# Low parts of the second feed-forward stage's down and plain weights: an adding transfer from GpSimd's queue instead of a VectorE subtraction

## The chip, the cores and the metric

The kernel runs on one core of a Trainium2 chip. The metric is the device time of one execution in microseconds. The kernel before took 1125.16 us (median of three runs, 1124.86 to 1127.51); lower is better.

## The reference

One step of a hybrid decoder layer in fp32, for 512 prompt tokens and 8 x 4 sample tokens that share all weights:

```
x = x + 1/2 * SwiGLU_1(RMSNorm(x))
h = RMSNorm(x); z = h @ w_in          # attention heads and mLSTM heads work on z
x = x + concat(A, B) @ w_out
x = x + 1/2 * SwiGLU_2(RMSNorm(x))

def _swiglu(x, w_gate, w_up, w_down):
    return (jax.nn.silu(x @ w_gate) * (x @ w_up)) @ w_down
```

The model width is 1024, the hidden width of the feed-forward stages 2816. The change lies in SwiGLU_2 alone, the last stage of the kernel.

## The kernel before

All activations are kept transposed: a tile holds 128 features in its partitions and all 544 tokens along its rows, in two halves of 272.

**Products in three passes.** To keep nearly fp32 accuracy with fast matrix products, every weight tile and every activation tile is split into a high part (rounded to the type fp32r) and a low part (the value less its high part). A product is then three matmul passes: high weight by high activation, high weight by low activation, low weight by high activation. The low part of the weights is read last of the three, for each of the (up to) eight blocks of 128 rows in turn.

**Raw tiles and jobs.** `Raw` (line 493) is one weight transfer from DRAM: eight blocks of 128 rows by 256 columns, 1 MB, into a tile `wraw` of which there are three buffers. It feeds two `Job`s (line 521), one for each 128 columns. `Job.split` (line 528) makes the two parts of its 128 columns: ScalarE casts to the high part `whi`, VectorE subtracts to get the low part `wlo`. Both come from one ring of eight buffers (`wsp`), so four jobs' weights fit. A job is then 48 matmuls (three passes, eight blocks, two halves of the tokens), 36 where it has six blocks.

**The second feed-forward stage** (`ffn_jobs`, line 717, called with "ffn2" at line 1803) goes through the 22 hidden blocks of 128 features in three parts of 8, 8 and 6 (`PARTS`, line 28). In each part, hidden blocks are made first (gate and up products, Silu, product), then added into all eight output blocks by eight down jobs. The first four hidden blocks (`PLAIN`, line 29) are made by plain jobs: two gate jobs and two up jobs for two blocks, eight jobs in all. All later ones are made by `Fast` jobs (line 555), a seven-product scheme on 2 x 2 blocks whose weight sums are made on VectorE; a fast job is seven units of 24 matmuls, each with its own split of weights, and has a separate loader and splitter. So the order of the stage is: eight plain jobs, two fast jobs, eight down jobs; four fast, eight down; three fast, eight down (six blocks each).

**What sets the order.** The program is written out by a planner at build time. `Order` (line 52) keeps a model clock of each engine and when each tile is ready; generators ("threads") are resumed when their model time has come, and emit their instructions. `run` (line 602) holds two of them: the loader, which issues the load of raw tile n on SP's queue when both jobs of raw tile n - 3 have been split, and the splitter, which splits a job's weights when TensorE is four units (two jobs) ahead of it, or three units where the job before is a fast one. Each engine then runs its own instructions in the order in which they were emitted, and waits on semaphores for what it needs. GpSimd issues nothing and computes nothing in this stage.

In the part that the change touches, the split reads:

```
src = self.raw.t[:, :nk, self.c * P:(self.c + 1) * P]
act.copy(hi[:, :nk], src)
yield R(hi) - 0.3
dve.tensor_tensor(lo[:, :nk], src, hi[:, :nk].bitcast(F32), op=OP.subtract)
self.raw.left -= 1
```

`yield R(hi) - 0.3` lets other threads go on until the model has `hi` ready.

Of the kernel before, what the change touches and what calls it, by code (L numbers as in the profile page):

```python
# [8 lines left out]
F32 = mybir.dt.float32  # L9
F32R = mybir.dt.float32r  # L10
AF = mybir.ActivationFunctionType
OP = mybir.AluOpType
# [4 lines left out]
P = 128  # L17
# [34 lines left out]
class Order:  # L52
# [26 lines left out]
    def done(self, *tiles, kind="aux"):  # L79
        for p in tiles:  # L80
            self.free[kind].append(self.used[p.tensor.name][0] + 0.2)
# [58 lines left out]
    def R(self, *aps):  # L140
        return max(self.ready.get(a.tensor.name, (0.0, ""))[0] for a in aps) + 0.2
# [103 lines left out]
def hybrid_layer_kernel(ctx: ExitStack, tc: tile.TileContext, I: dict, C: dict, O: list):  # L245
    nc = tc.nc
# [10 lines left out]
    od = Order()  # L257
    act, dve, pool = Engine(od, "act", nc.scalar), Engine(od, "dve", nc.vector), Engine(od, "pool", nc.gpsimd)
    dma = Engine(od, "dma", nc.sync)
    dma2 = pool  # L260
    R, U, done = od.R, od.U, od.done

    def halves(ap):
        return ap.rearrange("p (a b) -> p a b", a=2)
# [10 lines left out]
    def t2(name, shape=(P, N), dt=F32):  # L275
        return gp.tile(list(shape), dt, name=name, tag="t2", bufs=NT2)
# [33 lines left out]
    class Norm:  # L310
        def __init__(self, g0):
            self.g0 = g0
            self.x = [None] * KD
            self.begun = self.n = 0
            self.rows = False
            self.rb = None
# [49 lines left out]
    class FastNorm(Norm):  # L366
# [58 lines left out]
        def split(self, name, j, t):  # L425
            hi, lo = t2("oh", (P, 2, HN), F32R), t2("ol", (P, 2, HN), F32R)
            yield R(t) - 0.3
            act.copy(hi, t)
            yield R(hi) - 0.3
            dve.tensor_tensor(lo, t, hi.bitcast(F32), op=OP.subtract)  # L430
            self.ops[(name, j)] = (hi, lo)
# [61 lines left out]
    class Raw:  # L493


        def __init__(self, w, r0, nk, cols, *more):
            self.w, self.cols = w, cols
            self.parts = [(r0, nk)] + list(more)
            self.nk = sum(n for _, n in self.parts)
            self.left = len(cols)  # L500
            self.t = None

        def load(self):
            self.t = wp.tile([P, 8, 256], F32, name="wraw", tag="wraw", bufs=3)
# [1 line left out]

        def load_cols(self):
            c0, n = self.cols[0], len(self.cols)
            together = all(c == c0 + i * P for i, c in enumerate(self.cols))
            k0 = 0  # L510
            for r0, nk in self.parts:
                rows = self.w[r0:r0 + nk * P]
                if together:
                    dma.dma_start(self.t[:, k0:k0 + nk, :n * P], rows[:, c0:c0 + n * P].rearrange("(k p) c -> p k c", p=P))
                else:
                    for i, c in enumerate(self.cols):
                        dma.dma_start(self.t[:, k0:k0 + nk, i * P:(i + 1) * P],
                                      rows[:, c:c + P].rearrange("(k p) c -> p k c", p=P))
                k0 += nk

    class Job:
# [6 lines left out]
        def split(self):  # L528
            hi = wp.tile([P, 8, P], F32R, name="whi", tag="wsp", bufs=8)
            lo = wp.tile([P, 8, P], F32R, name="wlo", tag="wsp", bufs=8)  # L530
            nk = self.nk
            if self.custom:
                self.custom(hi, lo)
            else:
                src = self.raw.t[:, :nk, self.c * P:(self.c + 1) * P]
                act.copy(hi[:, :nk], src)
                yield R(hi) - 0.3
                dve.tensor_tensor(lo[:, :nk], src, hi[:, :nk].bitcast(F32), op=OP.subtract)
                self.raw.left -= 1
            self.w = (hi, lo)  # L540

# [175 lines left out]
    def ffn_jobs(pre, get_norm, after):  # L717
        wg, wu, wd = I[pre + "_w_gate"], I[pre + "_w_up"], I[pre + "_w_down"]
        jobs = []
        for f0, f1 in zip(PARTS, PARTS[1:]):  # L720
# [4 lines left out]
            def gate(f, zg=zg):  # L725
                def post(ps, full):
                    z = t2("zg")
                    yield 0, 0, lambda: get_norm().rb is not None
                    dve.tensor_tensor(halves(z), ps, halves(get_norm().rb), op=OP.mult)
                    done(full, kind="mm")  # L730
                    yield R(z) - 0.5
                    act.activation(z, z, AF.Silu)
                    zg[f] = z
                return post
# [9 lines left out]
            def up(f, zg=zg, hidden=hidden):  # L744
                def post(ps, full):
                    z = t2("zu")
                    yield 0, 0, lambda: zg[f] is not None
                    dve.tensor_tensor(halves(z), ps, halves(get_norm().rb), op=OP.mult)
                    done(full, kind="mm")
                    yield R(z) - 0.3  # L750
                    dve.tensor_tensor(z, zg[f], z, op=OP.mult)
                    yield from hidden(f, z)
                return post
# [63 lines left out]
            op = lambda name, k: get_norm().op(name, k)  # L817
            for f in range(0, nf, 2):
                c0 = (f0 + f) * P
                if f0 + f >= PLAIN:  # L820
                    jobs.append(Fast(Halves((wg, wu), 0, c0), Halves((wg, wu), 4 * P, c0), op, both(f)))
                    continue
                cols = [c0, c0 + P]
                ru = Raw(wu, 0, 8, cols)
                if jobs or f0 or f:
                    rg = [Raw(wg, 0, 8, cols)] * 2
                    jobs += [Job(rg[i], i, xs, gate(f + i)) for i in range(2)]
                else:
                    jobs += [Job(Raw(wg, 0, 8, [cols[i]]), 0, xs, gate(f + i)) for i in range(2)]
                jobs += [Job(ru, i, xs, up(f + i)) for i in range(2)]  # L830

            def down(m, last=f1 == NF):
                def post(ps, full):
                    dve.scalar_tensor_tensor(halves(xT[m]), ps, 0.5, halves(xT[m]), op0=OP.mult, op1=OP.add)
                    done(full, kind="mm")
                    if last:
                        yield from after(m)
                    yield 0
                return post

            for m in range(0, KD, 2):
                r = Raw(wd, f0 * P, nf, [m * P, (m + 1) * P])
                for c in range(2):
                    jobs.append(Job(r, c, lambda k, hs=hs: hs[k], down(m + c)))
        return jobs

    n1, n2, n3 = FastNorm(0), Norm(8), FastNorm(16)

    jobs = ffn_jobs("ffn1", lambda: n1, n2.add)

    last_fast = max(n for n, j in enumerate(jobs) if isinstance(j, Fast))
# [905 lines left out]
    for m in range(0, KD, 2):  # L1757
        r = Raw(w_out, 4 * P, 3, [m * P, (m + 1) * P])
        jobs += [Job(r, i, lambda k: mixed[4 + k], wo(m + i, False)) for i in range(2)]
    for m in range(0, KD, 2):  # L1760
        r = Raw(w_out, 0, 4, [m * P, (m + 1) * P], (7 * P, 1))
# [19 lines left out]
    def last_half(h, ps):  # L1781
# [19 lines left out]
        dma.dma_start(yp[:, 2 * h:2 * h + 2, m * P:(m + 1) * P], yt)  # L1801

    jobs += ffn_jobs("ffn2", lambda: n3, store)

    def late():
# [90 lines left out]
```

## Time and profile before

| | us |
|---|---|
| median of three runs | 1125.16 |
| the profiled execution | 1127.17 |
| its span, first to last instruction | 1125.4 |
| TensorE busy (matmul) | 1102.8 |
| VectorE busy | 768.4 |
| ScalarE busy | 504.3 |
| GpSimd busy | 95.6 |

The page and the views come from one profiled execution. PE is TensorE's matmuls and PEld its weight loads, DVE is VectorE, ACT ScalarE, POOL GpSimd, SP the engine that issues the loads; "SPq" marks such an issue, and its duration is the issue's own, not the transfer's. Nearly every instruction has line L223 or L282, the helpers that record it, so groups are told apart by the tiles that they write and read: `wlo<-wraw,whi` writes a low part from a raw tile and a high part. A bracket behind a row of a timeline is the idle time of the engine before it and who ended it. Matmuls are pipelined, so a single one lasts longer (about 0.29 us) than the step from one to the next (about 0.125 us).

### The profile page before, as it was taken

To read this page: it belongs to the slowest core of one execution; us is meant where nothing else is said; L and a number is where in the kernel's file an instruction comes from. 1 tells how busy PE (TensorE), PEld (TensorE's weight loads), DVE (VectorE), ACT (ScalarE), POOL (GpSimd) and SP (SyncE) were. 2 spreads that over 40 slices of the span, in tenths; PEclk is the share of its full clock that TensorE was granted. 3 is DMA by queue.
4 is the path that set the end of the run, shared out by engine and by line. 5 is a ranking of instruction groups with operands and counts; after the bars stand their busy time and mean duration, and the time that the engine had idled before them with its cause. 6 is when DMAs were issued, how large, how long until landed. Compare 5 with 4: busy or idle time off the path is not lost. (4 is left out here: it accounts for less than half of the span.)

```text
span 1125.4 us, 21401 instructions
## 1 busy us (share of the span) xinstructions
PE 1102.8 (98%) x8819; PEld 1050.6 (93%) x8819; DVE 768.4 (68%) x1232; ACT 504.3 (45%) x900; POOL 95.6 (8%) x105
## 2 busy tenths in 40 slices
PE   7999999999999999999989999999999999999998
PEld 6999999999999999988876869999999999999997
DVE  6888337873487678689786537778962687537752
ACT  5555215451245446455653535454541355314541
POOL 0000000000000000165563010000000000000000
PEclk9999999999999999999999999999999999999999
DMA  7305312432143465675979563342242122422232
GB/s 231 102 15 159 105 38 76 149 114 78 36 140 99 124 215 134 189 227 161 316 227 331 189 215 113 97 148 76 76 134 92 61 91 75 150 76 76 66 105 60
DMA packets 143229, 145.34 MB, mean 129 GB/s; under 512 B 8868, under 2 KB 120772, under 8 KB 143132
## 3 DMA queue, kind: packets, MB, share of 16 engines
q1 hardware_dynamic: 143068, 143.98, 41.2%
q8 instruction: 69, 1.13, 0.4%
q14 instruction: 28, 0.23, 0.1%
q0 software_dynamic: 64, 0.00, 0.0%
HBM read 132.54 MB, written 9.18 MB: 126 GB/s over the span
## 5 line engine op out<-in xcount | busy, mean ns | idle before, releaser
L223 ACT CAST whi<-wraw 128x1024 fp32r<-128x1024 f32 (+3 forms) x180 | 174.1, 988 | 121.0 <-PE mm L282 93.5
L223 DVE TENSOR_TENSOR wlo<-wraw,whi 128x1024 fp32r<-128x1024 f32 (+3 forms) x180 | 210.2, 1176 | 20.4 <-ACT whi L223 20.2
L282 PE MATMUL mm<-oh,wlo 128*128 128x272 f32 x720 | 209.3, 291 | 2.2 <-DVE wlo L223 2.0
L282 PE MATMUL mm<-oh,whi 128*128 128x272 f32 x720 | 207.6, 288 | 0.1
L282 PE MATMUL mm<-ol,whi 128*128 128x272 f32 x720 | 207.2, 288 | 0.0
L282 PE MATMUL mm<-xh,whi 128*128 128x272 f32 x720 | 157.8, 301 | 0.0
L282 PE MATMUL mm<-xh,wlo 128*128 128x272 f32 x720 | 149.5, 289 | 0.2 <-DVE wlo L223 0.2
L282 PE MATMUL mm<-xl,whi 128*128 128x272 f32 x720 | 149.5, 289 | 0.0
L282 PE MATMUL mm<-hh,whi 128*128 128x272 f32 x704 | 147.3, 289 | 0.5 <-DVE x L223 0.5
L282 PE MATMUL mm<-hh,wlo 128*128 128x272 f32 x704 | 146.4, 288 | 0.0
L282 PE MATMUL mm<-hl,whi 128*128 128x272 f32 x704 | 146.3, 288 | 0.0
L223 DVE SCALAR_TENSOR_TENSOR x<-mm,x 128x544 f32<-128x544 f32 (+1 forms) x49 | 34.9, 713 | 158.1 <-PE mm L282 158.1
L282 PEld LDWEIGHTS mm<-oh,wlo 128*128 128x128 f32 x720 | 135.4, 188 | 5.5 <-DVE wlo L223 4.4
L282 PEld LDWEIGHTS mm<-oh,whi 128*128 128x128 f32 x720 | 135.5, 188 | 0.3 <-issue 0.3
L282 PEld LDWEIGHTS mm<-ol,whi 128*128 128x128 f32 x720 | 135.6, 188 | 0.0
L282 PEld LDWEIGHTS mm<-xh,whi 128*128 128x128 f32 x720 | 112.8, 190 | 12.4 <-issue 11.4
L282 PEld LDWEIGHTS mm<-xh,wlo 128*128 128x128 f32 x720 | 113.6, 189 | 0.5 <-DVE wlo L223 0.5
L282 PEld LDWEIGHTS mm<-xl,whi 128*128 128x128 f32 x720 | 113.6, 189 | 0.1
L282 PEld LDWEIGHTS mm<-hh,whi 128*128 128x128 f32 x704 | 110.6, 188 | 0.9 <-DVE x L223 0.8
L282 PEld LDWEIGHTS mm<-hh,wlo 128*128 128x128 f32 x704 | 110.9, 188 | 0.0
L282 PEld LDWEIGHTS mm<-hl,whi 128*128 128x128 f32 x704 | 110.7, 188 | 0.0
L223 ACT CAST whi<-ws 128x1024 fp32r<-128x1024 f32 x54 | 56.7, 1051 | 104.1 <-DVE ws L223 104.0
(324 smaller groups left out, 1772.2 us busy)
## 6 DMA issues: line engine op xcount, KB each, us to landing
wraw<-in_ffn_w_gate_dram SPq DMA_DIRECT2D x40, 512.0 KB
wraw<-in_ffn_w_up_dram SPq DMA_DIRECT2D x36, 512.0 KB
wraw<-in_ffn_w_down_dram SPq DMA_DIRECT2D x16, 1024.0 KB
kv<-in_cache_k_win_dram SPq DMA_DIRECT2D x56, 256.0 KB
kv<-in_cache_v_win_dram SPq DMA_DIRECT2D x56, 256.0 KB
wraw<-in_w_in_dram SPq DMA_DIRECT2D x16, 512.0 KB
wraw<-in_ffn_w_down_dram SPq DMA_DIRECT2D x8, 768.0 KB
wraw<-in_w_in_dram SPq DMA_DIRECT2D x6, 1024.0 KB
```

The costliest lines, as they stand in the source:

```text
L223: r = fn(*args, **kw)
L282: nc.tensor.matmul(out, lhsT, rhs, start=start, stop=stop, **kw)
```

## The change

In the second feed-forward stage alone, the low part of every plain gate and up weight and of every down weight is made in another way: ScalarE writes the negated high part into `lo`, and a transfer issued from GpSimd's queue adds the raw weights onto it. The planner takes GpSimd for 1 us for this and has the low part ready 4 us after that. Fast jobs keep the VectorE subtraction, and so does every weight ahead of the second feed-forward stage.

So that the transfer reads whole rows, the two column blocks of such a raw tile are loaded into separate halves of the buffer (`apart`), by two DMAs with runs of 512 bytes instead of one with runs of 1 KB. Besides, the first two gate jobs of this stage, which had a raw tile each, now share one.

```
@@ Raw.load_cols
+            if self.sums:
+                flat = self.t.rearrange("p k c -> p (k c)")
+                self.apart = [flat[:, i * 8 * P:(i + 1) * 8 * P].rearrange("p (k c) -> p k c", k=8) for i in range(2)]
-            together = all(c == c0 + i * P for i, c in enumerate(self.cols))
+            together = not self.sums and all(c == c0 + i * P for i, c in enumerate(self.cols))
...
                     for i, c in enumerate(self.cols):
-                        dma.dma_start(self.t[:, k0:k0 + nk, i * P:(i + 1) * P],
+                        dma.dma_start(self.apart[i][:, k0:k0 + nk] if self.sums else self.t[:, k0:k0 + nk, i * P:(i + 1) * P],
                                       rows[:, c:c + P].rearrange("(k p) c -> p k c", p=P))
@@ Job.split
                 src = self.raw.t[:, :nk, self.c * P:(self.c + 1) * P]
+                if self.raw.apart:
+                    src = self.raw.apart[self.c][:, :nk]
                 act.copy(hi[:, :nk], src)
                 yield R(hi) - 0.3
-                dve.tensor_tensor(lo[:, :nk], src, hi[:, :nk].bitcast(F32), op=OP.subtract)
+                if self.raw.apart:
+                    act.activation(lo[:, :nk], hi[:, :nk].bitcast(F32), AF.Copy, scale=-1.0)
+                    yield R(lo) - 0.3
+                    nc.gpsimd.dma_start(lo[:, :nk], src, accum_op=OP.add)
+                    od.issue("pool", 1.0, [], [lo])
+                    t = max(od.t, od.clock["pool"]) + 4.0
+                    od.ready[lo.tensor.name] = od.used[lo.tensor.name] = od.used[src.tensor.name] = (t, "dma")
+                else:
+                    dve.tensor_tensor(lo[:, :nk], src, hi[:, :nk].bitcast(F32), op=OP.subtract)
                 self.raw.left -= 1
@@ ffn_jobs
                 ru = Raw(wu, 0, 8, cols)
-                if jobs or f0 or f:
+                ru.sums = pre == "ffn2"
+                if jobs or f0 or f or pre == "ffn2":
                     rg = [Raw(wg, 0, 8, cols)] * 2
+                    rg[0].sums = pre == "ffn2"
...
                 r = Raw(wd, f0 * P, nf, [m * P, (m + 1) * P])
+                r.sums = pre == "ffn2"
```

More of the change, by code (lines that the diff above doesn't have):

```diff
@@ L500, in __init__ @@
             self.left = len(cols)
-            self.t = None
+            self.t, self.apart, self.sums = None, None, False
         def load(self):
```

## The prediction

> **What bounds the kernel now.** I read the page's busy shares first, then the table of windows cut by stage, then the groups of instructions in the second feed-forward stage, and last the timelines around the places where a group of plain jobs begins.
>
> ```profile
> span 1125.4 us, 21401 instructions
> PE 1102.8 (98%) x8819; PEld 1050.6 (93%) x8819; DVE 768.4 (68%) x1232; ACT 504.3 (45%) x900; POOL 95.6 (8%) x105
> ```
>
> TensorE works for 98% of the span, so it is the bound, and taking work off VectorE (68%) is worth only what VectorE makes TensorE wait. The profiled execution took 1127.17 us, 1.8 us more than its span and 2.0 us more than the median of the three runs, 1125.16. About 0.3% of that, 3.4 us, is what a measurement of this kernel can tell from no change.
>
> How much TensorE waits in this stage is in the windows. The columns are the window, its length, then busy time and count for PE, PEld, DVE, ACT and POOL, the granted clock, the DMA engines' mean share and GB/s.
>
> ```profile
> 739.30:788.30 49.00, 49.00 (x391) 48.84 (x390) 40.10 (x63) 23.83 (x35) 0.00 (x0) 1.00 0.27 85
> ...
> 797.50:801.90 4.40, 3.38 (x27) 3.16 (x27) 3.92 (x5) 2.67 (x4) 0.00 (x0) 1.00 0.02 4
> ...
> 832.60:880.70 48.10, 48.10 (x386) 48.10 (x385) 17.07 (x19) 9.14 (x10) 0.00 (x0) 1.00 0.25 79
> ...
> 1117.90:1125.40 7.50, 2.73 (x22) 2.30 (x19) 0.72 (x2) 0.74 (x2) 0.00 (x0) 0.95 0.18 50
> sum 386.10, PE 378.68 PEld 375.58 DVE 245.07 ACT 156.24 POOL 0.00; mean PE 37.87 PEld 37.56 DVE 24.51 ACT 15.62 POOL 0.00
> ```
>
> From the first plain gate job at 739.3 to the end, TensorE is idle for 386.10 - 378.68 = 7.42 us. Of that, 7.50 - 2.73 = 4.77 us lie after 1117.9, in the last half tile's way out, where no weights are split any more. So 2.65 us is all that any relief of VectorE can bring. The eight plain jobs (739.3 to 788.3) and the first group of eight down jobs (832.6 to 880.7, 48.10 / 8 = 6.0 us a job) have no idle time at all: there the change can only add waits.
>
> **What is removed.** 32 subtractions leave VectorE: eight in the plain gate and up jobs, 24 in the three groups of down jobs, eight of these on three quarters of the width.
>
> ```profile
> L223 DVE TENSOR_TENSOR wlo<-wraw,whi 128x1024 fp32r<-128x1024 f32 x58 | 69.9, 1218 | 9.4 <-ACT whi L223 9.4
> L223 ACT CAST whi<-wraw 128x1024 fp32r<-128x1024 f32 x57 | 57.9, 1045 | 52.4 <-PE mm L282 41.9 <-issue 6.0 <-DVE wraw L223 3.7
> 799.00 0.39 PE L282 MATMUL aux<-oh,wlo 128*128 128x272 f32 x1 [1.02 <-DVE wlo L223]
> ```
>
> The first two rows are groups of the stage, the third is TensorE's timeline. 24 x 1.218 = 29.2 us and eight shorter ones leave VectorE, all of it beside TensorE's work. The one wait of size that VectorE causes is the third row: 1.02 us, in the first fast job behind the plain ones, for a low part that the change leaves on VectorE but that comes from a queue relieved of the plain jobs' subtractions. I take the whole 1.0 us as gain; its ends are 0, if VectorE's program order keeps it late, and the 2.65 us above.
>
> **What is added on ScalarE.** 32 negated copies, priced by the cast of the same size: 24 x 1.045 = 25.1 us and eight shorter ones. ScalarE is busy for 156 of the 386 us, so the sum is hidden, but each negation stands in its job's chain, between cast and transfer. Behind it on ScalarE wait at most a Silu or a cast of a hidden tile, one negation late, while VectorE, which finishes these tiles, is rid of a longer subtraction. I count nothing for that; without that cover it would be 1 us in each of three groups.
>
> **What is added on GpSimd's queue.** Per job one transfer of 512 KB from the raw tile, added onto the low part. The trace has no such transfer. Let L be the time from the end of the negation until TensorE may read the low part. How much L may be is read from the cast and from the first product with the low part. The rows give start and duration: the plain jobs first, then the three groups of down jobs, each with the cast of its first job and the product that needs it.
>
> ```profile
> 730.19 1.03 ACT L223 CAST whi<-wraw 128x1024 fp32r<-128x1024 f32 x1
> 739.79 0.29 PE L282 MATMUL mm<-xh,wlo 128*128 128x272 f32 x1
> 824.48 1.03 ACT L223 CAST whi<-wraw 128x1024 fp32r<-128x1024 f32 x1
> 826.68 1.05 ACT L223 CAST whi<-wraw 128x1024 fp32r<-128x1024 f32 x1 [1.16 <-PE mm L282]
> 833.11 0.41 PE L282 MATMUL mm<-hh,wlo 128*128 128x272 f32 x2
> 958.28 1.03 ACT L223 CAST whi<-wraw 128x1024 fp32r<-128x1024 f32 x1
> 966.88 0.29 PE L282 MATMUL mm<-hh,wlo 128*128 128x272 f32 x1
> 1070.85 0.82 ACT L223 CAST whi<-wraw 128x768 fp32r<-128x768 f32 x1
> 1079.46 0.41 PE L282 MATMUL mm<-hh,wlo 128*128 128x272 f32 x2
> ```
>
> With a negation as long as its cast, the slack is 739.79 - 732.25 = 7.54 us for the first plain job, 833.11 - 826.54 = 6.57, 966.88 - 960.34 = 6.54, and 1079.46 - 1072.49 = 6.97 for the first jobs of the down groups. The second job of the first down group (cast at 826.68, needed 6.0 us after 833.11) has 10.3 us. So four places decide, and above all the three starts behind fast jobs, where weights are split three units ahead and not four.
>
> Now L, from three sets of rows: the only transfers that GpSimd issues in this kernel (two tiny ones), the DMA engines in three windows, and one pair of loads with the VectorE instruction that waited for it.
>
> ```profile
> L223 POOL DMA_DIRECT2D out_dram<-mrow x2: 671/777/883, 428.8 to 434.2; - x2
> DMA to landing us min/median/max: 4.7/5.5/6.3
> 715.75:718.16 2.41, 2.41 (x22) 2.41 (x21) 1.19 (x2) 0.56 (x2) 0.00 (x0) 1.00 0.75 221
> 829.00:831.00 2.00, 2.00 (x18) 2.00 (x17) 1.85 (x4) 0.59 (x2) 0.00 (x0) 1.00 0.97 336
> 936.26 0.37 SPq L223 DMA_DIRECT2D wraw<-in_ffn_w_gate_dram  x1
> 936.67 0.50 SPq L223 DMA_DIRECT2D wraw<-in_ffn_w_up_dram  x1
> 941.92 1.23 DVE L223 TENSOR_TENSOR ws<-wraw 128x1024 f32<-128x1024 f32 x1 [0.25 <-DMA wraw<-in_ffn_w_up_dram]
> ```
>
> Transfers of next to nothing, issued by GpSimd, took 4.7 to 6.3 us to land. That they write to DRAM and this one to SBUF may make them too dear; that they carry nothing makes them too cheap. The lower end for L is therefore 4.7 us, as if the data cost nothing. One 512 KB load, alone, keeps the engines at 0.75 for 2.41 us. The adding transfer must read the raw tile and the negated copy, 1 MB, and write 512 KB: up to twice 2.41, and on top of 6.3 that is the upper end, 6.3 + 4.8 = 11.1 us. Between them lies the nearest row by bytes: the gate and up pair, 1 MB, issued at 936.26 and used at 941.92, took 5.66 us on SP's queue. GpSimd needs 0.78 us to issue where SP needs 0.37, and the window at 829 shows the engines taken to 0.97 by the down loads just when the first group's transfer would run, which can add up to the 2.0 us of that window: 6.1 to 8.1. I take 7.9, towards its upper end, because the down loads also become pieces of 512 bytes; it is also the middle of 4.7 and 11.1.
>
> The reading of two sources has a rule. The Trainium skill (Collectives: The Full Stack, "The bandwidth ceiling: the fold count and why AG ≠ RS ≠ AR") says that a transfer that adds is slow not for the sum but because two source reads share one read ring, and reaches about half the rate of a copy. It speaks against this change, and no run here shows it yet. By it the data term is the 4.8 us and not the 2.4 us of a copy, and with L at about 9 the waits below come to 7.5 us and the time to 1131.7.
>
> At L = 7.9 the waits are 7.9 - 7.54 = 0.4 in the plain group, 1.3 and 1.4 in the first two down groups, and in the third, with a quarter less data (0.9 us of the 3.6 between the two readings 2.4 and 4.8), 7.0 - 6.97 = 0.0. Together 3.1 us, less the 1.0 us gained: +2.1 us.
>
> **What moves with it.** A raw buffer is now free when the transfer has landed and no longer when VectorE has read it, about 7.7 us later (negation plus 7.9 less 1.2), and SP's queue holds every later load behind that wait.
>
> ```profile
> 823.63 6.59 SPq L223 DMA_DIRECT2D wraw<-in_ffn_w_down_dram  x3
> 840.74 0.37 SPq L223 DMA_DIRECT2D wraw<-in_ffn_w_gate_dram  x1
> ...
> 857.50 1.22 DVE L223 TENSOR_TENSOR wlo<-wraw,whi 128x1024 fp32r<-128x1024 f32 x1
> 875.56 1.22 DVE L223 TENSOR_TENSOR wlo<-wraw,whi 128x1024 fp32r<-128x1024 f32 x1
> ```
>
> The third of these down loads starts at about 830 and feeds the split at 857.50; the next one, at 840.74, feeds that of 875.56. Eight microseconds later, both are still over 15 us early. Nothing else is queued on SP there. Loads in two halves of 512-byte pieces cost more engine time, 2.41 us per 512 KB against 9.8 us for three megabytes of the same stage's loads in 1 KB pieces at most:
>
> ```profile
> 824.70:834.50 9.80, 9.80 (x80) 9.80 (x80) 7.84 (x12) 5.07 (x8) 0.00 (x0) 1.00 0.95 322
> ```
>
> That is 4.8 instead of 3.3 us a megabyte; at a mean share of 0.25 in the down jobs it is hidden, and at the group starts it is in the 7.9. The first two gate columns become one raw tile, so the following up tile is loaded a buffer earlier; nothing waits for it now, and I count nothing.
>
> **The sum.** On the profiled execution's own time: 1127.17 + 3.1 - 1.0 = 1129.3. On the median: 1125.16 + 2.1 = 1127.3 us, which counts as no change.
>
> **The rivals.** *The transfer is late at every group start* (chance 0.32). Half shares with the down loads at 0.97 and two readings bring L to 9.5 to 11.1; at 10.3 the four waits are 2.8, 3.7, 3.8 and 2.4, 12.7 us in all, and the time is 1125.16 + 12.7 - 1.0 = 1136.9. It decides from L = 8.2 on, where the sum passes 3.4 us. For it: the share of 0.97. Against: the pair's 5.66.
>
> *GpSimd is held while it writes its descriptors* (0.09).
>
> ```profile
> L223 POOL TENSOR_TENSOR hf<-hf,mo 128x544 f32<-128x544 f32 x3 | 5.8, 1927 | 1.7 <-ACT hf L223 1.7
> L223 POOL TENSOR_TENSOR qw<-mq,W 128x544 f32<-128x544 f32 x4 | 5.4, 1354 | 24.6 <-DVE mq L223 9.6 <-PE aux L282 8.9 <-DVE sden L223 4.3
> ```
>
> The same shape takes GpSimd 1.35 or 1.93 us: something in this kernel makes it wait. If the issue waits for one VectorE pass of 1.22 us, L is 9.1 and the waits are 1.6, 2.5, 2.6 and 1.2: 7.9 - 1.0 = +6.9, 1132.1. The Trainium skill (SBUF — State Buffer, "Who interferes with whom") says that VectorE and GpSimd share a pair of SBUF ports and that whichever issues second is blocked whole, descriptor writing included when VectorE is in a two-port mode. For an operation with two SBUF inputs, which nearly all of VectorE's here are, it expects no hold on descriptors, so by the page this rival is unlikely.
>
> *The transfer is slower than a job* (0.07). Above 6.0 us of engine time each, transfers queue behind one another and every job is late. At 8 us it would cost 2 us in each of 31 jobs, about 1187 us.
>
> *VectorE was holding more than it shows* (0.04): the 2.65 us and something of the tail go, about 1121.5.
>
> **How the numbers follow.** The forecast (L from 4.7 to 8.2: -1.0 to +3.4 us, so 1124.2 to 1128.6) has 0.48. Slower by over 0.3% is 0.32 + 0.09 + 0.07 = 0.48, the same weight; faster is 0.04. The forecast stays the likeliest single case. The range goes from 1124.0 to 1138.0: it leaves out the slow transfer, the upper part of the first rival and the gain.
>
> **What would show it.** Right: the transfer's L near 8 us, waits of TensorE of 1 to 2 us "<-DMA wlo" in front of the first product with a low part at the starts of the first two down groups and next to none elsewhere, VectorE about 37 us less busy, ScalarE about 32 us more, the 1.02 us wait gone. Wrong: waits inside the groups (the rate), over 2 us at each start (L), a low part that waits for GpSimd's own issue, or a wait of a cast for a raw load.

## The result, and the profile after

The changed kernel takes 1132.86 us (median of five runs, 1130.42 to 1136.16) against 1126.04 for the kernel before in the same five rounds: 1.0063 of it, with a 95% interval of 1.0041 to 1.0085. That is slower, by 4.6 to 9.6 us. The profiled execution took 1132.86 us with a span of 1130.7, 5.3 us more than the span before. The lines of its page that answer to those of before, and the new transfers (count, size, median time from issue to landing):

```profile
span 1130.7 us, 21539 instructions
PE 1102.7 (98%) x8819; PEld 1049.8 (93%) x8819; DVE 735.7 (65%) x1200; ACT 535.1 (47%) x932; POOL 122.8 (11%) x137
...
q0 software_dynamic: 4672, 15.73, 7.6%
...
wlo<-wraw POOLq DMA_DIRECT2D x24, 512.0 KB, 6.9
wlo<-wraw POOLq DMA_DIRECT2D x8, 384.0 KB, 5.5
```

The change does what it says: 32 transfers from GpSimd's queue, VectorE 32.7 us less busy, ScalarE 30.8 us more. TensorE does the same work in the same time, so the 5.3 us are waits. The windows, cut at the same places of the program, say where (columns as in the prediction: length, then busy time of PE first). The second and the third group of down jobs before:

```profile
966.40:1014.40 48.00, 48.00 (x386) 48.00 (x385) 17.08 (x19) 9.13 (x10) 0.00 (x0) 1.00 0.25 79
...
1079.00:1117.90 38.90, 38.37 (x310) 38.06 (x310) 12.42 (x17) 10.48 (x22) 0.00 (x0) 1.00 0.18 53
```

The stage after the change:

```profile
739.80:789.10 49.30, 49.30 (x391) 48.92 (x390) 33.98 (x58) 30.63 (x42) 5.78 (x7) 1.00 0.68 161
...
798.10:802.40 4.30, 3.36 (x27) 3.14 (x26) 3.82 (x5) 2.65 (x4) 0.00 (x0) 1.00 0.01 4
...
833.10:883.20 50.10, 48.38 (x387) 48.16 (x386) 9.97 (x13) 15.37 (x16) 5.09 (x6) 1.00 0.71 167
...
969.20:1020.20 51.00, 48.44 (x387) 48.22 (x386) 10.01 (x13) 15.37 (x16) 5.08 (x6) 1.00 0.71 165
1020.20:1084.70 64.50, 64.04 (x507) 63.41 (x506) 49.26 (x59) 35.01 (x51) 1.70 (x2) 1.00 0.32 92
1084.70:1123.60 38.90, 38.37 (x310) 38.06 (x310) 6.90 (x11) 15.54 (x28) 5.09 (x6) 1.00 0.64 141
```

The first down group grew from 48.10 to 50.10 us and the second from 48.0 to 51.00: 5.0 us of the 5.3. The third did not change (38.90 both times), the plain jobs by 0.3 us. Half a microsecond of the 5.3 lies ahead of the stage, which begins at 739.8 instead of 739.3. In each of the two groups it is one wait, in front of the first product with a low part. TensorE's timeline there:

```profile
833.32 0.41 PE L282 MATMUL mm<-hl,whi 128*128 128x272 f32 x2
835.46 0.52 PE L282 MATMUL mm<-hh,wlo 128*128 128x272 f32 x2 [1.72 <-DMA wlo<-wraw]
...
969.45 0.41 PE L282 MATMUL mm<-hl,whi 128*128 128x272 f32 x2
972.42 0.52 PE L282 MATMUL mm<-hh,wlo 128*128 128x272 f32 x2 [2.56 <-DMA wlo<-wraw]
```

A wait takes some tenths more from the group than its own length: pairs of matmuls that follow one another begin every 0.25 us and last 0.41, so the last pair ends 0.16 us after the next could have begun, and the first pair behind a wait lasts 0.52. The chain ahead of the first of them, from ScalarE's and GpSimd's timelines and the landing of that one transfer:

```profile
824.97 1.03 ACT L223 CAST whi<-wraw 128x1024 fp32r<-128x1024 f32 x1
826.04 1.06 ACT L223 ACTIVATE wlo<-whi 128x1024 fp32r<-128x1024 f32 x1
```

```profile
827.39 0.84 POOL L546 DMA_DIRECT2D wlo<-wraw  x1 [52.61 <-ACT wlo L223]
```

```profile
L546 POOL DMA_DIRECT2D wlo<-wraw x1: 842/842/842, 827.4 to 827.4; - x1
...
DMA to landing us min/median/max: 8.0/8.0/8.0
```

Negation done at 827.10, issue at 827.39, landed 8.02 us later at 835.41, product at 835.46. The same view gives 8.8 us for the first transfer of the second group, 6.5 for the third, and 4.6 us where nothing else is loaded, as for the last down job of the first group. So a transfer takes 4.6 us alone, and nearly twice that where it matters. The packets of the trace split it: alone, the first of its 4 KB rows moves 1.4 us after the issue, and it lands 3.2 us behind that; in the two groups the first row moves 3.5 and 3.9 us after the issue, and it lands 4.5 and 5.0 us behind that. The second and the third raw tile of down weights are being loaded just then, and the engines are full (the experiments below ask whether that is the cause):

```profile
825.20:835.40 10.20, 8.53 (x68) 8.31 (x66) 5.85 (x10) 7.48 (x11) 1.70 (x2) 1.00 1.09 270
```

A DMA share over 1 means that the times of packets overlap. It takes no second queue for that: with the narrow loads alone, and no transfer from GpSimd, the share at these loads is 1.14 (below).

### The profile page after: what moved, and what is told of

Its sections match the earlier page's. It is cut to its first block, busy times and chain, and to the rows that moved or that the text cites. A ratio compares the mean times of both kernels' runs of the same rounds, so it can differ in the third digit from the quotient of the medians.

```text
span 1130.7 us, 21539 instructions
## 1 busy us (share of the span) xinstructions
PE 1102.7 (98%) x8819; PEld 1049.8 (93%) x8819; DVE 735.7 (65%) x1200; ACT 535.1 (47%) x932; POOL 122.8 (11%) x137
## 5 line engine op out<-in xcount | busy, mean ns | idle before, releaser
L223 DVE TENSOR_TENSOR wlo<-wraw,whi 128x1024 fp32r<-128x1024 f32 (+3 forms) x148 | 173.6, 1183 | 20.2 <-ACT whi L223 19.8
```

Source lines behind the costliest of these rows:

```text
L223: r = fn(*args, **kw)
```

## The experiments

Theory A: the change costs only the two waits, because the first transfer of a down group lands late, and it lands late because of the loads that run beside it. Rival B: transfers and negations cost a little everywhere. Rival C: the loads in 512-byte runs cost time by themselves. All eight kernels were timed in five rounds beside the kernel before (its medians: 1126.48 beside the first four, 1127.78 beside the others).

**The first job of each down group on VectorE again.**

```
-                if self.raw.apart:
+                if self.raw.apart and not self.first:      # first: job 0 of a down group
                     act.activation(lo[:, :nk], hi[:, :nk].bitcast(F32), AF.Copy, scale=-1.0)
```

> The first job of each of the three down groups gets its low part from VectorE again; all 29 other transfers, the negations and the narrow loads stay. Theory A (the change costs only the two waits of 1.7 and 2.6 us for the first low part of the first two down groups): both waits are gone, the second job's transfer lands about when it is needed (9.2 us after its issue in the changed kernel, 9.3 us of slack), so at most a few tenths are left; the span falls by 4 to 5 us to about 1126, ratio 0.999 to 1.002. Rival B (the transfers or negations cost a little everywhere, the waits are only where it shows): 29 of 32 remain, so at least 1.0045. Rival C (the loads in 512-byte runs cost it): they are all still there, 1.005 or more.

Ratio 1.0003 (0.9994 to 1.0012), 1126.54 us. No wait for a transfer is left, and the two groups are back at their length before:

```profile
833.58:881.70 48.12, 48.12 (x386) 48.12 (x385) 10.00 (x13) 15.37 (x16) 5.09 (x6) 1.00 0.67 161
967.40:1015.62 48.22, 48.22 (x387) 48.22 (x385) 10.02 (x13) 15.38 (x16) 5.08 (x6) 1.00 0.67 162
```

29 of 32 transfers, their negations and all narrow loads are still there and cost nothing that can be told (at most 0.0012 of the time, 1.4 us): B and C fall.

**Low products last in that job.**

```
+            if isinstance(j, Job) and j.first:
+                for w, part in ((hi, (0, 1)), (lo, (0,))):
+                    for k in ks: ...                       # all high-weight products, then all low ones
```

> As the changed kernel, but the first job of each down group takes its high-weight products for all its blocks first and the low-weight products last: the low part is needed 4.0 us after the job's start and not 0.5 us, 3.5 us later, and nothing else moves. Theory A: waits of 1.7 and 2.6 us are covered, ratio 0.999 to 1.002; a small new wait (under 1 us) may come for the last hidden tiles, which are now needed 1.5 us earlier. Rival B (cost everywhere) and rival C (narrow loads): no change against the changed kernel, 1.005 or more.

1.0013 (1.0003 to 1.0022), 1128.12 us. The transfers land as late as before (8.0 and 8.7 us), but the waits for them are gone, by moving only the moment of need. A new one of 0.24 us for a hidden tile's low part stands in the third group, which was foreseen. The group takes 39.77 us instead of 38.90, half of the 1.6 us between the medians; the rest stays unexplained. On ScalarE the hidden tile's cast stands behind a weight's cast and a negation, the delay that the prediction named and counted as nothing; in the changed kernel nobody waits for it, here the tile is needed earlier:

```profile
1079.73 0.83 ACT L223 CAST whi<-wraw 128x768 fp32r<-128x768 f32 x1
1080.60 0.85 ACT L223 ACTIVATE wlo<-whi 128x768 fp32r<-128x768 f32 x1
1081.35 0.63 ACT L223 CAST hh<-zu 128x544 fp32r<-128x544 f32 x1
```

**The third raw tile held back until the first transfer has landed.**

```
+                    if getattr(r, "gate", None):           # third raw tile of a down group
+                        yield 0, 0, lambda: r.gate.w is not None
+                        dma.dma_start(gate_d[0:1], r.gate.w[1][0:1, 0, 0:8].bitcast(F32))
                     r.load()
```

> As the changed kernel, but in each down group SP's queue first stores eight numbers of the first job's low part, and only then loads the third raw tile: that 1 MB is off the DMA engines until the first transfer has landed. Theory A with contention (a transfer alone takes 4.6 us from issue to landing, 8.0 and 8.8 where loads run): landing falls from 8.0 and 8.8 to 5.5 to 6.5 us, the waits to 0 to 0.5 us each, ratio 0.999 to 1.003. Rival A' (the start of the transfer on GpSimd's queue is late in itself behind fast jobs, not because of loads): landing stays at 8 and the ratio at 1.005.

1.0000 (0.9991 to 1.0009), 1126.31 us. Nothing of the transfer was touched, only a load that stood beside it, and it lands 3.2, 3.1 and 1.7 us earlier in the three groups. The first transfer of the first and of the second group:

```profile
L546 POOL DMA_DIRECT2D wlo<-wraw x1: 842/842/842, 826.1 to 826.1; - x1
...
DMA to landing us min/median/max: 4.8/4.8/4.8
```

```profile
L546 POOL DMA_DIRECT2D wlo<-wraw x1: 844/844/844, 959.9 to 959.9; - x1
...
DMA to landing us min/median/max: 5.7/5.7/5.7
```

Its first row moves 1.4 us after the issue, as when alone. So the late start is the load's doing and not GpSimd's, whose issue takes 0.84 us in both kernels, behind an idle time as long. By what way the load holds the transfer up is not shown. Later transfers of the same group, now beside the held load, need up to 10.5 us, and nobody waits for them.

**Wide loads.**

```
-                self.apart = [flat[:, i * 8 * P:(i + 1) * 8 * P].rearrange("p (k c) -> p k c", k=8) for i in range(2)]
-            together = not self.sums and all(c == c0 + i * P for i, c in enumerate(self.cols))
+                self.apart = [self.t[:, :, i * P:(i + 1) * P] for i in range(2)]
+            together = all(c == c0 + i * P for i, c in enumerate(self.cols))
```

> As the changed kernel, but the raw tiles are loaded as before (one load, runs of 1 KB), and the transfer reads runs of 512 bytes of them. Loads take 3.3 us a megabyte and not 4.8, so the engines are free earlier at the group starts; the transfer's own pieces become eight times as many. If the narrow loads make the contention, landing falls from 8.0 and 8.8 to about 7 us and the waits to 0.5 to 1.5 us, ratio about 1.003. If short pieces cost the transfer more than that (piece by piece the 512-byte loads took 27 ns against 46 ns for 1 KB, so up to a fifth more, 0.6 us), landing stays at 8 to 9 and the ratio at 1.005 to 1.007.

1.0085 (1.0072 to 1.0098), 1137.37 us: worse than both guesses. A 512-byte piece of an adding transfer takes 68 ns (median of the trace's packets), so 512 KB needs 64 x 68 = 4.4 us an engine, where eight rows of 4 KB need 8 x 328 = 2.6. GpSimd's issue grows to 1.5 us. Landing takes 9.2 and 8.7 us, and now all four starts wait; the granted clock falls in the groups:

```profile
739.54 0.52 PE L282 MATMUL mm<-xh,wlo 128*128 128x272 f32 x2 [1.95 <-DMA wlo<-wraw]
...
837.27 0.82 PE L282 MATMUL mm<-hh,wlo 128*128 128x272 f32 x2 [2.97 <-DMA wlo<-wraw]
...
976.59 0.82 PE L282 MATMUL mm<-hh,wlo 128*128 128x272 f32 x2 [2.49 <-DMA wlo<-wraw]
...
1092.83 0.52 PE L282 MATMUL mm<-hh,wlo 128*128 128x272 f32 x2 [1.82 <-DMA wlo<-wraw]
```

```profile
833.64:887.73 54.09, 51.12 (x387) 50.90 (x385) 10.03 (x13) 15.36 (x16) 9.22 (x6) 0.94 0.89 151
837.20:841.20 4.00, 3.93 (x17) 3.93 (x18) 0.00 (x0) 1.47 (x2) 2.90 (x2) 0.50 1.08 121
```

The first group is 6.0 us longer for a wait of 2.97, because behind the wait the clock was granted at 0.50. Laying the halves apart was thus right. Beside the wide loads the first piece of a group's first transfer still moved 3.8 and 3.9 us after the issue, 2.1 us where nothing was loaded: 1.7 and 1.8 us late, against 2.1 and 2.5 beside the narrow loads. So wide loads delay the start too; how much the narrow ones add is not told apart by this run, since its transfers differ as well.

**The narrow loads alone, and the plain jobs alone.** In the first the loads of the change stay and all low parts come from VectorE; in the second `r.sums = pre == "ffn2"` is taken away from the down tiles.

> Only the loads of the change (column blocks in separate halves, two DMAs with runs of 512 bytes, one gate tile for two jobs); the low parts come from VectorE as before. Theory A (the first transfers of the first two down groups land late): no transfer, no wait, ratio 0.999 to 1.001. Rival C (the narrow loads cost time by themselves): 1.003 or more.

> Only the eight plain gate and up jobs take the transfer; the 24 down jobs are as before. Theory A: the plain jobs had no wait in the changed kernel (first landing 4.6 us after issue, 7 us of slack), so the ratio is 0.999 to 1.001, and the wait of 0.94 us in the first fast job stays, because VectorE is busy there with the fast job's own work. If relief of VectorE were worth its 1 us, the span would be about 1 us shorter and that wait gone. Rival B (cost everywhere): a quarter of the cost, 1.001 to 1.002.

0.9994 (0.9983 to 1.0005) and 0.9994 (0.9986 to 1.0003): neither costs anything nor gains anything that can be told. The narrow loads do hold the DMA engines longer (share 1.14 with them, 0.91 before, in the same window), and nobody waits for that:

```profile
824.00:834.00 10.00, 10.00 (x82) 10.00 (x81) 8.04 (x12) 5.29 (x9) 0.00 (x0) 1.00 1.14 295
```

The wait in the first fast job, which the relief of VectorE was to end, is 1.02 us with the first and 0.94 with the second:

```profile
799.87 0.40 PE L282 MATMUL aux<-oh,wlo 128*128 128x272 f32 x1 [0.94 <-DVE wlo L223]
```

**Copying instead of adding.** `accum_op=OP.add` is taken away. This kernel leaves the high part out of the difference, so its low products are made with the raw weights.

> As the changed kernel, but the transfer copies the raw weights into the low part instead of adding them, so the high part is left out of the difference and the low products are not the right ones; issue, size and places are the same. It measures what the adding costs. If the adding reads two sources one after the other, a 4096-byte row takes about 165 ns in place of 328 (the kernel's 2 KB loads took 84 ns), and a transfer alone lands in 1.4 + 1.4 + 0.35 = 3.2 us and not 4.6. At the down groups, where the start is delayed to 3.5 and 3.9 us by the loads, landing falls from 8.0 and 8.8 to about 6 to 6.7, the waits to 0 to 0.6 us, ratio 0.999 to 1.002. If the adding is free and the contention alone counts, rows stay at 328 ns or landing at 8, and the ratio at 1.005.

0.9999 (0.9988 to 1.0011), 1126.92 us. A 4 KB row takes 182 ns (median) and not 328, and a transfer alone lands in 2.9 us. Beside the loads it starts at 3.15 us and lands at 5.9 and 7.1; one wait of 0.86 us is left in the second group, none in the first. Alone the copy's first row moves after 1.1 us. So both parts of the delay count: the start behind the loads (2 us), which a copy has too, and the adding (1.7 us of 4.6 alone, 2.1 and 1.7 in the two groups).

**Two halves.**

```
+                    for k0, k1 in ((0, 4), (4, nk)):
+                        nc.gpsimd.dma_start(lo[:, k0:k1], src[:, k0:k1], accum_op=OP.add)
+                        od.issue("pool", 1.0, [], [lo])
```

> As the changed kernel, but each transfer goes in two of half the rows each, the first four blocks first (two issues of 0.85 us on GpSimd). Theory A: the first half has half the bytes to move behind the loads; it lands about 1.4 to 2 us earlier than the whole did, 6 to 7 us after its issue, and the waits fall from 1.7 and 2.6 us to 0 to 1 us, ratio 1.000 to 1.003. If the start behind the loads is the whole delay (3.5 to 3.9 us to the first packet, whatever the size), or the second half takes turns with the first, landing stays near 8 and the ratio at 1.005.

1.0010 (0.9997 to 1.0023), 1129.19 us. The first halves land 6.8 and 6.5 us after their issue, where the wholes took 8.0 and 8.8, and the waits fall from 1.72 and 2.56 us to 0.64 and 0.29:

```profile
833.89 0.49 PE L282 MATMUL mm<-hh,wlo 128*128 128x272 f32 x2 [0.64 <-DMA wlo<-wraw]
...
968.25 0.49 PE L282 MATMUL mm<-hh,wlo 128*128 128x272 f32 x2 [0.29 <-DMA wlo<-wraw]
```

No version is faster than the kernel before. None can be by much: in the stage only about 2.65 us of TensorE's idle time lay ahead of its end.

## Why the prediction was right or wrong, point by point

- *The bound.* Right. TensorE's busy time did not move, 32.7 us less on VectorE and 30.8 more on ScalarE changed nothing by themselves, and 29 of the 32 transfers cost nothing that can be told. (The low parts' rows add up to 210.2 us before and 173.6 after, the 37 us less of the prediction; neighbouring instructions overlap, so the busy time falls by 32.7.)
- *The gain of 1.0 us.* Wrong: 0.08, so the end of 0 that was named held. The wait at 799 went from 1.02 to 0.94. VectorE's timelines show why. Before, the last subtraction of the plain jobs begins at 771.11, and VectorE then idles three times for want of other engines, the last time ahead of 782.48:

```profile
771.11 1.22 DVE L223 TENSOR_TENSOR wlo<-wraw,whi 128x1024 fp32r<-128x1024 f32 x1
...
782.48 0.72 DVE L223 TENSOR_TENSOR zu<-mm,rb 128x544 f32<-128x544 f32 x1 [1.68 <-PE mm L282]
```

  After, it idles at the same place, and from there to the low part that TensorE waits for it is busy for 16.03 of 16.15 us with work that the change leaves to it:

```profile
783.28 0.72 DVE L223 TENSOR_TENSOR zu<-mm,rb 128x544 f32<-128x544 f32 x1 [1.74 <-PE mm L282]
783.92 1.22 DVE L223 TENSOR_TENSOR wlo<-wraw,whi 128x1024 fp32r<-128x1024 f32 x1
...
798.21 1.22 DVE L223 TENSOR_TENSOR wlo<-ws,whi 128x1024 fp32r<-128x1024 f32 x1
```

```profile
799.48 0.39 PE L282 MATMUL aux<-oh,wlo 128*128 128x272 f32 x1 [0.94 <-DVE wlo L223]
```

  The splitter lets the fast job's splits start only when TensorE is within two or three units, so time freed earlier cannot be spent on them. VectorE does have too much to do there, but none of what was removed lies in that stretch, and the rows of before showed it already.
- *Where it waits.* Right for the two groups: the starts behind fast jobs, and there only. In the changed kernel the slack from the end of the negation is 833.57 - 827.10 = 6.47 us, against 6.57 in the prediction. In the plain group it was not 7.54: the negation was emitted behind two operations of the norm, at 734.50, and the low part came at 740.45 for a product due at 740.33. It cost little (the plain jobs grew by 0.3 us), because no load was beside it.
- *L.* The value, 7.9 us, was about right for the first group (835.46 - 827.10 = 8.4) and too small for the second (972.42 - 963.24 = 9.2). Taking one value for all four places was the mistake: it was 5.0 us in the plain group. The ends 4.7 and 11.1 held all of it. That 7.9 came near 8.4 is partly luck, for two terms were off in opposite ways. The base of 6.1 us, from the pair of loads, was too dear: 0.3 us to the issue and 4.6 to the landing, 4.9 in all. The up to 2.0 us for the loads beside it were too cheap: 8.0 - 4.6 = 3.4 and 8.8 - 4.6 = 4.2.
- *The two readings.* A row takes 328 ns added and 182 copied, 1.8 times as long. The Trainium skill ("The bandwidth ceiling: the fold count and why AG ≠ RS ≠ AR" in Collectives: The Full Stack) gives about half the rate for the adding step of a collective; the ratio agrees, and that two reads share a ring is not shown here. The data term was sized wrongly even so: eight rows an engine are 8 x 328 = 2.6 us added and 1.5 copied, not 4.8 and 2.4. That the time by that rule, with L at about 9, lies near the result is luck too: the loads beside the transfers took the time that the rule had put down to the data.
- *The sum.* +2.1 us forecast, +5.3 in the profile and +6.8 by the medians. That it counts as no change was wrong: the whole interval, 4.6 to 9.6 us, lies above the 3.4 us. The missing parts are 0.9 us of gain that did not come, 0.4 and 1.2 us of wait in the two groups (1.72 and 2.56 for 1.3 and 1.4), and some 0.7 us that the two groups lost beyond the waits' own length, which the working left out. (The 0.5 us ahead of the stage belong to none of them, so that the parts need not close to a tenth.) What came is the first rival's mechanism, from its threshold of 8.2 us on, at half of its places; its price of 12.7 us was for all four and for L of 10.3. The range held because it took in the lower part of this rival; the forecast by itself did not hold.
- *GpSimd held at its issue.* Did not happen: in the down groups every issue began 0.29 us after its negation and took 0.84 to 0.86 us, whether VectorE was idle (at 836.40) or at an operation with two SBUF inputs (`hl<-zu,hh` at 1087.15). The Trainium skill ("Who interferes with whom" in SBUF — State Buffer) expects no hold for such operations; the trace agrees.
- *Loads behind later buffers.* Right: no cast waited for a raw tile.

The medians' 6.8 us is more than the profiles' 5.3 mainly because of the executions that were profiled. That of the changed kernel took 1132.86 us, which is its median; that of the kernel before took 1127.17, 1.1 us above its median of 1126.04. The other 0.4 us lie outside the spans. The runs of the changed kernel also spread over 5.7 us where those of before in the same rounds spread over 2.7, and its two slowest (1133.93 and 1136.16) have a mean granted clock of 0.995. Waits that sometimes are long enough to lower the clock, as in the run with wide loads, would explain that; it was not shown for this kernel.

## What to carry to other kernels

When work moves from an engine to a queue, price the delay at the place with the least slack and with what else is on the DMA engines at that moment, not on average: here 29 transfers cost nothing that can be told, and two cost 5.0 of the 5.3 us. Three things brought the time back to that of before, or nearly, without touching the engines' work: need the late operand later (order of the products), send the part that is needed first, or hold back the load that stands in its way. And before you count a wait for an engine as a gain, look at the busy stretch that ends in the wait, and whether the work that you remove lies in it.

## What the runs showed of the hardware that was not expected

- A transfer from GpSimd's queue starts late beside a full load stream: its first row moved 3.5 and 3.9 us after the issue instead of 1.4, the copy's 3.15 instead of 1.1. With one load held back it was 1.4 again.
- An adding transfer's 512-byte piece costs 68 ns, and 4 KB in one row 328: by the byte 1.7 times as much.
- GpSimd's issue took different times by what was issued: 0.53 us for the copy, 0.84 for the addition, 1.5 with eight times as many pieces.
- In the wide-loads run TensorE's waits of 1.95, 2.97 and 2.49 us were followed by a granted clock of 0.50 for 3.4, 6.8 and 3.4 us; its wait of 1.82 us, and those of 1.72 and 2.56 in the changed kernel's profile, were not. So the length of a wait alone did not decide it in these runs.
